# Log-softmax over 50,000 columns: straight code for 512 tiles turned into a hardware loop of 62 rounds over eight fixed buffers

## The chip, the cores and the metric

One core of one Trainium2 chip. The time is that of one execution on the device, in microseconds (us); the core's span in the profile is some 2 us shorter.

## The reference

```
x: [16, 512, 50000] float32
max_x   = max(x, last axis);  shifted = x - max_x
out     = shifted - log(sum(exp(shifted), last axis))
```

8192 rows of 50,000 numbers are read once and written once: 1638 MB in and 1638 MB out. The kernel takes 16 rows as one tile, each row cut into eight pieces, so a tile is 128 partitions x 6250 numbers (3.2 MB); there are 512 tiles.

## The kernel before

The parts that matter, shortened (cuts marked with `...`, loops over halves written in words):

```
NBUF = 8; AHEAD = 7
data = tile_pool(bufs=NBUF)                       # eight buffers of [128, 6250]

def load(t):
    buf = data.tile([P, W]);  nc.sync.dma_start(out=buf, in_=xt[t])          # SP's queue
def front(t):
    nc.vector.reduce_max(out=pmax, in_=buf)       # then four small VectorE steps: row maximum
    ...
    nc.scalar.activation(Exp, two halves of 3125, accum_out=part)            # ScalarE
    nc.tensor.matmul(rowsum, ones, part)          # sum over the eight pieces of a row
    nc.scalar.activation(out=logsum, in_=rowsum, func=Ln)
def back(t):
    nc.vector.tensor_scalar(out=buf, in0=buf, negmax, logsum, add, subtract) # in place
    nc.scalar.dma_start(out=ot[t], in_=buf)                                  # ScalarE's queue

for t in range(AHEAD): load(t)
for t in range(ntiles + 1):
    front(t); back(t - 1); load(t + AHEAD)        # each where it exists
```

VectorE, ScalarE, TensorE and SP are engines of the core, each with a stream of instructions of its own. SP issues the loads and ScalarE the stores; a DMA engine then moves the bytes, and the transfer has landed when its semaphore, a counter that others wait on, has its full count. A store's issue stands in ScalarE's instruction stream, so if it has to wait, ScalarE waits with it.

## Time and profile before

| | before |
|---|---|
| time, median of 6 runs (spread) | 7614.2 us (7614.0 to 7616.0) |
| per tile (span / 512) | 14.87 us |
| DMA share in the middle, GB/s | 1.00, 433 |
| load / store, issue to landing | 51.9 / 37.5 us |
| VectorE, ScalarE busy | 73%, 41% |

In the profile, "DMA share" is the mean busy share of the sixteen DMA engines, and "us to landing" runs from the instruction that issues a transfer to the semaphore that tells of its end. The lines are in the prediction below. The trace also holds a record of every DMA packet (start, length, queue, size), from which I take what no view prints: q1 carries the loads, q10 the stores, packets of 4 bytes, sixteen for each transfer, are the completion writes.

### The profile page before, as it was taken

How to read it: one execution, taken by the hardware profiler on the slowest of the kernel's cores; microseconds unless marked ns; L12 is line 12 of the kernel's file. 1: busy time of each engine (PE TensorE's matmuls, PEld its weight loads, DVE VectorE, ACT ScalarE, POOL GpSimd, SP SyncE). 2: the span in 40 equal slices, each digit the busy share in tenths (PEclk: the TensorE clock that was granted, in tenths of full speed). 3: DMA queues.
4: the chain of work that ended last, by engine and by line, in shares of the span. 5: the costliest groups of instructions: out<-in, count | busy, mean ns of one | idle time of the engine just before them, and what ended most of it. 6: DMA issues, size and time to landing. Idle time of an engine off the chain costs nothing.

```text
span 7612.6 us, 12833 instructions
## 1 busy us (share of the span) xinstructions
PE 600.6 (8%) x2048; PEld 513.2 (7%) x2048; DVE 5567.2 (73%) x3072; ACT 3153.1 (41%) x2561; POOL 1.2 (0%) x7
## 2 busy tenths in 40 slices
PE   0000000000000000000000000000000000000000
PEld 0000000000000000000000000000000000000000
DVE  7777777777777777777777777777777777777776
ACT  4444444444444444444444444444444444444443
POOL 0000000000000000000000000000000000000000
DMA  9999999999999999999999999999999999999998
GB/s 425 433 432 432 432 432 432 432 432 432 432 432 432 432 432 432 432 432 432 432 432 432 432 432 432 432 432 432 432 432 432 432 432 432 431 432 432 432 432 380
DMA packets 147540, 3277.68 MB, mean 431 GB/s; under 512 B 16384, under 2 KB 16384, under 8 KB 16384
## 3 DMA queue, kind: packets, MB, share of 16 engines
q1 hardware_dynamic: 73728, 1638.43, 50.0%
q10 hardware_dynamic: 73728, 1638.43, 50.0%
q14 instruction: 68, 0.56, 0.0%
q8 instruction: 16, 0.26, 0.0%
HBM read 1638.40 MB, written 1638.40 MB: 430 GB/s over the span
## 4 chain that ended last, share of the span: by engine, by line
DVE 73%; another core or an unknown queue 25%; issue 1%; DMA 0%; ACT 0%; PE 0%; ACTq 0%
DVE pmax L81 45%; DVE buf L117 23%; DVE allmax L84 1%; DVE rowmax L86 1%; DVE spread L91 1%; DVE negmax L96 0%; DMA buf<-in_x_dram 0%; ACT dump L102 0%; PE rowsum L108 0%; ACT logsum L112 0%; ACTq L102 0%
## 5 line engine op out<-in xcount | busy, mean ns | idle before, releaser
L81 DVE TENSOR_REDUCE pmax<-buf 128x1 f32<-128x6250 f32 x512 | 3411.8, 6664 | 1953.7 <-DMA buf<-in_x_dram 1953.7
L102 ACT ACTIVATE dump<-buf,negmax 128x3125 f32<-128x3125 f32 x1024 | 2938.1, 2869 | 4092.9 <-DVE negmax L96 4029.5
L117 DVE TENSOR_SCALAR buf<-buf,negmax,logsum 128x6250 f32<-128x6250 f32 x512 | 1789.7, 3496 | 4.5 <-ACT logsum L112 3.6
L108 PE MATMUL rowsum<-part,ones 128*128 128x1 f32 x2048 | 600.6, 363 | 6991.7 <-ACT dump L102 6991.7
L108 PEld LDWEIGHTS rowsum<-part,ones 128*128 128x128 f32 x2048 | 513.2, 311 | 7079.0 <-ACT dump L102 7057.2
L112 ACT ACTIVATE logsum<-rowsum 128x1 f32<-128x1 f32 x512 | 87.6, 171 | 345.8 <-PE rowsum L108 345.8
L102 ACT ACTIVATION_READ_ACCUMULATOR dump<-buf,negmax 128x1 f32 x1024 | 191.1, 187 | 0.0
L96 DVE STREAM_TRANSPOSE negmax<-spread 128x32 f32<-128x32 f32 x512 | 108.2, 211 | 17.7
L84 DVE STREAM_TRANSPOSE allmax<-pmax 128x32 f32<-128x32 f32 x512 | 108.3, 211 | 17.4
L86 DVE TENSOR_REDUCE rowmax<-allmax 128x4 f32<-128x32 f32 x512 | 95.3, 186 | 17.7
L91 DVE COPY spread<-rowmax 128x32 f32<-128x32 f32 x512 | 92.9, 181 | 17.8
L67 ACT ACT_TABLE_LOAD x1 | 1.3, 1283 | 0.8 <-PEq L146 0.8
L59 POOL TENSOR_SCALAR_AFFINE_SELECT ones<-ones 128x128 f32<-128x128 f32 x1 | 0.4, 403 | 0.1
L63 POOL TENSOR_SCALAR_AFFINE_SELECT ones<-ones 128x128 f32<-128x128 f32 x1 | 0.4, 397 | 0.1
L57 POOL MEMSET ones<- 128x128 f32 x1 | 0.2, 204 | 0.3 <-POOLq L146 0.3
L146 POOL MEMSET const-bfloat16-1.0<- 128x1 bf16 x1 | 0.1, 101 | 0.0
L146 POOL MEMSET const-uint8-127<- 128x1 uint8 x1 | 0.1, 101 | 0.0
L146 POOL MEMSET const-float32-0.0<- 128x1 f32 x1 | 0.1, 98 | 0.3 <-issue 0.3
L146 POOL MEMSET const-float32-1.0<- 128x1 f32 x1 | 0.1, 98 | 0.0
## 6 DMA issues: line engine op xcount, KB each, us to landing
buf<-in_x_dram SPq DMA_DIRECT2D x512, 3125.0 KB, 51.9
out_dram<-buf ACTq DMA_DIRECT2D x512, 3125.0 KB, 37.5
```

Of the source, the lines that this page charges most:

```text
L59: nc.gpsimd.affine_select(out=ones3, in_=ones3, pattern=[[-G, R], [0, G]], base=0, channel_multiplier=1, compare_op=ALU.is_ge, fill=0.0,)
L63: nc.gpsimd.affine_select(out=ones3, in_=ones3, pattern=[[G, R], [0, G]], base=G - 1, channel_multiplier=-1, compare_op=ALU.is_ge, fill=0.0,)
L67: nc.scalar.preload_act_table_set("natural_log_exp_and_others")
L81: nc.vector.reduce_max(out=pmax, in_=buf, axis=AX)
L84: nc.vector.transpose(out=allmax, in_=pmax.to_broadcast([P, SQ]))
L86: nc.vector.tensor_reduce(out=rowmax, in_=allmax.rearrange("p (r g) -> p r g", g=G), op=ALU.max, axis=AX, negate=True,)
L91: nc.vector.tensor_copy(out=spread.rearrange("p (r g) -> p r g", g=G), in_=rowmax[:, :, None].to_broadcast([P, SQ // G, G]),)
L96: nc.vector.transpose(out=negmax, in_=spread)
L102: nc.scalar.activation(out=dump, in_=buf[:, j * EXP_C : (j + 1) * EXP_C], func=ACT.Exp, bias=negmax[:, 0:1], scale=1.0, accum_out=part[:, ...
L108: nc.tensor.matmul(rowsum, ones, part[:, j : j + 1], start=j == 0, stop=j == nexp - 1)
L112: nc.scalar.activation(out=logsum, in_=rowsum, func=ACT.Ln)
L117: nc.vector.tensor_scalar(out=buf, in0=buf, scalar1=shift.pop(t)[:, 0:1], scalar2=logs.pop(t), op0=ALU.add, op1=ALU.subtract,)
```

## The change

The intent is a short program: one copy of eight tiles' instructions in a loop, in place of 512 copies, without a barrier between rounds. Its core (the tiles' code moves unchanged, with fixed buffers and single small tiles in place of pools):

```diff
-    data = ... bufs=NBUF        stats = ... bufs=4
+    bufs  = [data.tile([P, W], name=f"buf{j}") for j in range(NBUF)]
+    shift, logs = one small tile per buffer;  pmax, allmax, ... one each
+    def dram(a, t):
+        return a[bass.ds(t, 1)].rearrange("o p w -> (o p) w")     # t may be a register
...
-        nc.sync.dma_start(out=buf, in_=xt[t])
+        nc.sync.dma_start(out=bufs[j], in_=dram(xt, t))
...
-        nc.scalar.dma_start(out=ot[t], in_=buf)
+        nc.scalar.dma_start(out=dram(ot, t), in_=buf)
...
+    def round_of(t, first=False, last=False):
+        for j in range(NBUF):
+            front(j)
+            ...
+            back((j - 1) % NBUF, t + j - 1)
+            load((j - 1) % NBUF, t + j - 1 + NBUF)                # not past the end
-    for t in range(ntiles + 1): ...
+    round_of(0, first=True)
+    with tc.For_i(NBUF, ntiles - NBUF, NBUF, iteration_sync="reg_based") as t:
+        with tc.manual_schedule():
+            round_of(t)
+    round_of(ntiles - NBUF, last=True)
+    back(NBUF - 1, ntiles - 1)
```

## The prediction

> **What bounds the kernel now.** I read the page first: the line of DMA busy tenths, the table of queues, the costliest groups and the DMA issues.
>
> ```profile
> DMA  9999999999999999999999999999999999999998
> q1 hardware_dynamic: 73728, 1638.43, 50.0%
> q10 hardware_dynamic: 73728, 1638.43, 50.0%
> ...
> L81 DVE TENSOR_REDUCE pmax<-buf 128x1 f32<-128x6250 f32 x512 | 3411.8, 6664 | 1953.7 <-DMA buf<-in_x_dram 1953.7
> L102 ACT ACTIVATE dump<-buf,negmax 128x3125 f32<-128x3125 f32 x1024 | 2938.1, 2869 | 4092.9 <-DVE negmax L96 4029.5
> L117 DVE TENSOR_SCALAR buf<-buf,negmax,logsum 128x6250 f32<-128x6250 f32 x512 | 1789.7, 3496 | 4.5 <-ACT logsum L112 3.6
> ...
> buf<-in_x_dram SPq DMA_DIRECT2D x512, 3125.0 KB, 51.9
> out_dram<-buf ACTq DMA_DIRECT2D x512, 3125.0 KB, 37.5
> ```
>
> Loads (q1) and stores (q10) each take 50.0% of the sixteen DMA engines: together all of them, for the whole span. 7612.6 us / 512 tiles is 14.87 us a tile, in which one load and one store of 3.2 MB move. VectorE needs 6.66 + 3.50 us and four small instructions of about 0.2 us, 10.9 us a tile; ScalarE 2 x 2.87 us and small change, about 6.5. Both wait. A load is on its way for 51.9 / 14.87 = 3.5 tiles and a store for 37.5 / 14.87 = 2.5: the DMA engines are full because several transfers stand in each queue at all times.
>
> The waits of the load queue, and a window in the middle, come next:
>
> ```profile
> SPq L75 <- DMA out_dram<-buf: 7305.6, 504, 26.8
> ...
> 4000.00:4100.00 100.00, 7.61 (x26) 6.50 (x26) 73.69 (x42) 42.55 (x33) 0.00 (x0) 1.00 1.00 433
> ```
>
> The load queue always waits for a store to land, since a load takes the buffer of a store. The window's last columns (DMA share 1.00, 433 GB/s) show no idle DMA.
>
> The DMA packet records in the trace give the grain: each transfer is 8 packets of 25,000 bytes on each of 16 engines, a packet takes 928 ns, and a busy engine alternates between q1 and q10. Sixteen packets are 16 x 0.928 = 14.85 us, which is the pace.
>
> Last, how long a transfer takes outside of moving data, from the first load, the first store and the tail (timeline, and the view of the output tensor in the window of the first store):
>
> ```profile
> 0.81 82.23 SPq L75 DMA_DIRECT2D buf<-in_x_dram  x11
> 11.05 6.66 DVE L81 TENSOR_REDUCE pmax<-buf 128x1 f32<-128x6250 f32 x1 [11.05 <-DMA buf<-in_x_dram]
> ```
>
> ```profile
> L121 ACTq DMA_DIRECT2D out_dram<-buf x1: 374/374/374, 32.9 to 32.9; - x1
> ...
> DMA to landing us min/median/max: 20.1/20.1/20.1
> ```
>
> ```profile
> 7592.47 4.05 ACTq L121 DMA_DIRECT2D out_dram<-buf  x2
> ```
>
> The first load, alone, took 11.05 - 0.81 = 10.24 us for 8 x 0.928 = 7.42 us of packets (a cold start). The first store, alone in its queue against a backlog of loads, took 20.1 us. In the tail, with idle engines, the store issued at 7592.47 has its first packet at 7593.31 in the packet records: 0.84 us. The first load's last completion is at 10.68 there and SP issues on it at 11.05; the first store's at 52.74, and SP issues at 53.13: a sequencer reacts to a landing in about 0.4 us.
>
> **What the Trainium skill says.** "DMA: Bandwidth & Descriptors", section "Queues, rings and completion order": an engine round-robins between queue rows at packet granularity. The packet records agree, q1 and q10 alternate. The same page, "Anatomy of one DMA", fits about 2.0 us of fixed cost per transfer (on the GpSimd path) and says that engines never wait on semaphores, the issuing sequencer does. Here I measure 0.84 + 0.4 = 1.24 us warm and 2.8 cold. "Runtime: NRT & Kernel Launch", section "Instruction fetch mechanics": a branch out of the fetched blocks of 256 instructions stalls. No loop body here has 256 instructions on an engine, and ScalarE and VectorE have slack, so no stall should show. "Advanced Engine Details and Errata", "Control Flow Timing", gives about 108 ns for a compare-and-branch; this trace has no branch to check it, and 62 of them are under 7 us even if nothing hid them.
>
> **The change part by part.** The arithmetic, the tile order and the look-ahead (load of tile t+8 once the store of t has landed) are the same. Three things differ.
>
> (1) Loop control: register arithmetic before most waits, and 62 branches per engine. It lies in VectorE's 4 us and ScalarE's 8 us of slack per tile. Instruction fetch falls away (68 packets of 8 KB before). I count 0 us.
>
> (2) Waits on stores. This decides. I read the built program's instruction order with its waits. Before, a store waits for its data and for the store four tiles earlier (the semaphore it reuses). In the loop, the output address comes from a register, and each store waits for the one just before it. The listing on ScalarE, with thresholds from the program:
>
> ```
> store tile t-1 : waits DMAHW0,2,4,6 (all stores of earlier rounds); raises DMAHW0
> store tile t   : waits DMAHW0 >= base+16 (store t-1 landed); raises DMAHW2
> store tile t+1 : waits DMAHW2 >= base+16 (store t landed);   raises DMAHW4
> store tile t+2 : waits DMAHW4 >= base+16; raises DMAHW6
> ```
>
> So only one store is ever in flight, where there were 2.5, and ScalarE, which issues them, stands at each wait.
>
> What a tile then takes: a store lands; ScalarE issues the next store and SP issues a load (it waits for the same landing). Each reaches the engines after 0.4 + 0.84 = 1.24 us. By then the load queue is empty, as I argue: a store now takes longer than 14.85 us from issue to issue, loads get packets in turn with it and all of the gap, so per tile they could move more than the one load that is added; the 3.5 loads of backlog are used up in some ten tiles and the loaded tiles pile up in the buffers. Then one load and one store start together on idle engines and share them, 16 packets, 14.85 us; the store's completion write also has to wait its turn behind the load's last packet. Sum: 1.24 + 14.85 = 16.09 us. I add 0.3 us for what starting from idle costs, my choice: the first load's first packets took 1.3 to 2.3 us instead of 0.93, and packets of engines that start in step took 0.93 to 0.97. That gives 16.4 us a tile. Nothing else is on this path: after issuing a store, ScalarE runs the next tile's exponentials, matmul wait and logarithm in about 7 us while the store flies; VectorE's 10.9 us also fit.
>
> The loop has 62 x 8 = 496 stores. Tile 7's store, the loop's first, should land near 161 us as before (in the old kernel tile 502's landed at 7511, 495 tiles of 14.85 earlier is 161). 161 + 495 x 16.4 = 8279. Some 20 us more for the tiles whose store runs against a backlog (20.1 as the first store did). So the loop's last store lands near 8299.
>
> (3) The loop's end. SP waits there for every transfer of the loop, then all engines meet in a barrier. The last load starts when the last store has landed: 0.4 + 0.84 + 7.5 = 8.7 us with all engines idle, and I allow 3 us for the barrier: 8311. Then eight tiles are left, seven loaded, at VectorE's pace (after the first tiles of the old kernel, 40.37 - 29.45 = 10.92): the maximum of tile 511 is ready after 7 x 10.92 + 7.5 = 84 us. From there the old kernel took 7612.6 - 7585.4 = 27 us to its end, with a straggling DMA engine; I take 23. Total 8311 + 84 + 23 = 8418, rounded to 8400.
>
> **The rivals.** *The loop is free:* the waits on the previous store are met in time, the queues stay full, only the drain at the end costs. Old pace, load 510 issued at 7511, 3.5 loads drain in 26 us, barrier 3, then 84 + 23: about 7650. For it: the DMA engines do the same work, and the change was meant to do this. Against it: stores took 37.5 us at one every 14.87; with one in flight that pace is only possible if a store takes under 14.87 from issue to next issue, and 16 packets alone are 14.85. *The loads fill the gap:* some backlog of loads stays, or stores reach the engines ahead of loads, so that one load packet runs in the gap of 1.24 us: 16.4 - 0.93 = 15.5 us, about 7970. Round-robin with a completion write that waits its turn speaks against it; that both are released by the same landing leaves the order open. *Fixed costs are larger:* 2.0 us as the skill's fit or 2.8 as in the cold first load, 16.9 to 17.7 us a tile: 8650 to 9050. For it: register-addressed transfers may be slower to start, which the old trace can't show; against it the warm 0.84 and 0.4. *ScalarE becomes serial* (exponentials wait for the store too, about 23 us a tile, over 11,000): the order says otherwise, as they come after the issue, not after the landing.
>
> **Range and chances.** The tile time is worth 495 us per us. From 15.7 (gap partly filled) to 17.2 us: 8060 to 8800. The free loop, or a nearly full gap, is all that gives less than 2%; I put 8% on it. Faster by 2% is barred by 512 x 14.85 = 7603 us of packets: 1%.
>
> **What would show it.** In the changed profile: ScalarE's queue waiting for stores to land about 500 times, 8 us or so each; store issue to landing about 16 us in place of 37.5, load about the same in place of 51.9; DMA share about 0.90 and near 390 GB/s all through; VectorE's idle time ended by ScalarE's logarithm, not by loads; VectorE and ScalarE instructions of unchanged length; an end of some 110 us with stores alone. A DMA share of 0.99 in the middle would prove the serial stores harmless, and idle time at each eighth tile alone would mean that the loop's edge, not the store chain, costs.

## The result, and the profile after

9413.7 us median of 6 runs (9407.6 to 9417.2): 1.236 times before, 95% interval 1.235 to 1.238. Ratios in this document are the mean time of one kernel's runs over the mean of the other's runs of the same rounds, so not quite the ratio of the medians. Executions over 1.5% slower than the fastest of the same kernel are left out of the means. The direction and the path were right; the time lies far above the stated range of 8060 to 8800.

The page of the changed kernel, the lines that answer to those of before (busy us and mean ns, then idle time before them and what ended it):

```profile
DMA  9888888888888888888888888888888888888887
...
q1 hardware_dynamic: 73728, 1638.43, 46.6%
q10 hardware_dynamic: 73728, 1638.43, 41.4%
...
L112 DVE TENSOR_SCALAR buf<-buf,negmax,logsum 128x6250 f32<-128x6250 f32 x512 | 1809.2, 3534 | 3623.4 <-ACT logsum L108 3623.4
L87 DVE TENSOR_REDUCE pmax<-buf 128x1 f32<-128x6250 f32 x512 | 3407.7, 6656 | 113.4 <-PEq L162 55.1
...
buf<-in_x_dram SPq DMA_DIRECT2D x512, 3125.0 KB, 18.1
out_dram<-buf ACTq DMA_DIRECT2D x512, 3125.0 KB, 18.3
```

Three things to see. The DMA engines have idle time everywhere, not in one place. Each instruction is as long as before (6656 ns against 6664, 3534 against 3496), so no engine got slower. And VectorE no longer waits for loads (113 us of idle time before its maximum, whatever ended it, against 1953.7): it waits for ScalarE's logarithm. Loaded tiles are there and nobody can go on. A load or a store now lands after 18 us, where they took 51.9 and 37.5: queues that used to hold several transfers hold one.

A window in the middle (the last two columns are DMA share and GB/s):

```profile
4000.00:4100.00 100.00, 5.87 (x20) 5.01 (x20) 60.90 (x35) 31.15 (x26) 0.00 (x0) 1.00 0.86 341
```

One period of the timeline (start, length, engine, line, instruction, idle time before it):

```profile
4006.59 37.41 SPq L83 DMA_DIRECT2D buf<-in_x_dram  x3
4006.61 0.36 ACTq L116 DMA_DIRECT2D out_dram<-buf  x1
4007.23 2.87 ACT L100 ACTIVATE dump<-buf,negmax 128x3125 f32<-128x3125 f32 x1 [11.72 <-DVE negmax L98]
...
4013.92 0.17 ACT L108 ACTIVATE logsum<-rowsum 128x1 f32<-128x1 f32 x1 [0.68 <-PE rowsum L105]
4014.12 3.54 DVE L112 TENSOR_SCALAR buf<-buf,negmax,logsum 128x6250 f32<-128x6250 f32 x1 [7.55 <-ACT logsum L108]
4017.57 6.66 DVE L87 TENSOR_REDUCE pmax<-buf 128x1 f32<-128x6250 f32 x1
...
4025.21 0.36 ACTq L116 DMA_DIRECT2D out_dram<-buf  x1
```

A load and a store leave together at 4006.6; ScalarE does its 7 us of work and is done at 4014.1; then it does nothing until the next store leaves at 4025.21. Note how the profile names the 11.72 us before the exponentials: "DVE negmax". That is the last semaphore the exponentials themselves waited for. What really held ScalarE is the wait in front of the store that stands ahead of them in its stream, and a wait for a landing ahead of a DMA issue is in no engine's busy time. The Trainium skill says something near: "Perfetto Trace Analysis", section "Summary: the profiler window per engine type", has the data movement of a DMA outside the window reported for its instruction. This trace agrees for the instruction (0.36 us for a transfer that takes 18.3), and shows the movement all the same, in the packet records.

Those records tell what the 18.6 us from 4006.6 to 4025.2 are. The old store's last completion write is at 4005.97, the new issues at 4006.6. The sixteen engines begin from 4007.54 on with a load packet each, which takes 2.04 us on the mean in place of 0.93; the first store packets start at 4009.55. From there on load and store packets take turns at 0.93 us. The store's sixteen completions come between 4023.58 and 4024.58.

### The profile page after: what moved, and what is told of

It reads as the page before. It is cut to its first block, busy times and chain, and to the rows that moved or that the text cites. A ratio compares the mean times of both kernels' runs of the same rounds, so it can differ in the third digit from the quotient of the medians.

```text
span 9410.8 us, 21999 instructions
## 1 busy us (share of the span) xinstructions
PE 598.8 (6%) x2048; PEld 513.1 (5%) x2048; DVE 5576.6 (59%) x3072; ACT 3152.2 (33%) x2561; POOL 1.2 (0%) x7
## 5 line engine op out<-in xcount | busy, mean ns | idle before, releaser
L112 DVE TENSOR_SCALAR buf<-buf,negmax,logsum 128x6250 f32<-128x6250 f32 x512 | 1809.2, 3534 | 3623.4 <-ACT logsum L108 3623.4
L87 DVE TENSOR_REDUCE pmax<-buf 128x1 f32<-128x6250 f32 x512 | 3407.7, 6656 | 113.4 <-PEq L162 55.1
L89 DVE STREAM_TRANSPOSE allmax<-pmax 128x32 f32<-128x32 f32 x512 | 108.2, 211 | 17.7
## 6 DMA issues: line engine op xcount, KB each, us to landing
out_dram<-buf ACTq DMA_DIRECT2D x512, 3125.0 KB, 18.3
```

Of the source, the lines that this page charges most:

```text
L87: nc.vector.reduce_max(out=pmax, in_=buf, axis=AX)
L89: nc.vector.transpose(out=allmax, in_=pmax.to_broadcast([P, SQ]))
L112: nc.vector.tensor_scalar(out=buf, in0=buf, scalar1=shift[j][:, 0:1], scalar2=logs[j], op0=ALU.add, op1=ALU.subtract,)
```

## The experiments

I took each period apart in the packet records and issue times (means over tiles 60 to 439, a period being from one store's last completion to the next's; for the loads alone, from load to load):

| us per tile | predicted | changed kernel | e2 straight chain | e4 late load | e7 stores alone | e8 loads alone |
|---|---|---|---|---|---|---|
| landing to next issue | 0.40 | 0.66 | 0.60 | 0.44 | 0.50 | 0.44 |
| issue to that transfer's first packet | 0.84 + 0.93 | 2.87 | 2.88 | 2.64 | 1.17 | 0.94 |
| first packet to its first completion | 13.92 | 14.05 | 14.03 | 11.16 | 7.40 | 8.07 |
| first to last of its 16 completions | 0.30 | 0.85 | 0.83 | 1.58 | 0.35 | 0.91 |
| sum = period | 16.4 | 18.42 | 18.34 | 15.82 | 9.42 | 10.36 |
| first load packet of an engine | 0.93 | 2.01 | 2.00 | 0.99 | - | 1.66 |

(The prediction's sum is split as it was meant: the load's first packet ahead of the store, then fifteen packets; its 0.30 was one lump for starting from idle.)

### The loop with free stores

```diff
+        if not isinstance(t, int): loop_stores.append(...)     # the eight stores of the loop body
...
         with tc.manual_schedule():
             round_of(t)
+        for i, late in enumerate(loop_stores):
+            for early in loop_stores[:i]:
+                tc.declare_no_dep(late, early, query=ANY_SYNC, reason="other rows of out")
+            for other in loop_stores:
+                tc.declare_no_dep(late, other, query=ANY_SYNC, across_iterations=True, reason=...)
```

> The loop as it is, with the store-after-store waits taken out: the eight stores of a round are declared independent of each other, within a round and across rounds (they write different rows), so a store waits only for the store four earlier whose semaphore it reuses, as in the straight kernel. Theory S (each store waits for the one before to land, and that alone costs): about 7655 us, 7635 to 7690; the pace is 14.85 us a tile again, the rest is the drain at the loop's end. Rival L (loop control, register arithmetic, register-addressed transfers cost): stays near 9400 us.

Measured: 7645.2 us, 1.0041 of before (1.002 to 1.006), correct. A fourth run of 7822.3 was slow and isn't used. In the built program each store of the loop again waits only for its data and the store four earlier. The page's DMA issues and the same window:

```profile
buf<-in_x_dram SPq DMA_DIRECT2D x512, 3125.0 KB, 24.0
out_dram<-buf ACTq DMA_DIRECT2D x512, 3125.0 KB, 59.3
```

```profile
4000.00:4100.00 100.00, 7.63 (x27) 6.55 (x27) 73.18 (x42) 42.91 (x34) 0.00 (x0) 1.00 1.00 432
...
7480.00:7520.00 40.00, 0.00 (x0) 0.00 (x0) 0.00 (x0) 0.00 (x0) 0.00 (x0) 1.00 0.70 284
7520.00:7560.00 40.00, 1.76 (x6) 1.50 (x6) 24.32 (x13) 12.13 (x9) 0.00 (x0) 1.00 0.43 172
```

A store takes 59.3 us, four periods, so four are in flight; the DMA engines are full again at 1.00. The loop, its registers and its branches are all still there and cost nothing that shows in the pace. The last two lines are the loop's end: all compute stands still while SP waits for the last transfers, then the DMA engines run short. In the same two windows the kernel before had a DMA share of 1.01 and 0.94.

### The straight kernel with chained stores

```diff
+LANDED = DependencyInfo(DependencyClass.Sync, DependencyReason.DATA)
...
-        nc.scalar.dma_start(out=ot[t], in_=buf)
+        st = nc.scalar.dma_start(out=ot[t], in_=buf)
+        if 7 <= t <= 502:
+            tc.add_manual_dep(st, stores[t - DEPTH].name, LANDED, ...)   # DEPTH = 1
+        stores[t] = st
```

> The straight kernel of before with one thing added: from tile 7 to tile 502 each store waits until the store before it has landed. No loop, no registers. Theory S: about 9400 us, 9250 to 9500 (18.5 us a tile, as in the changed kernel's trace, and no drain). Rival L: 7614 us, unchanged.

Measured: 9323.8 us, 1.2245 of before. No loop, and nearly the whole loss: 1710 of 1800 us. Its issues on the page:

```profile
buf<-in_x_dram SPq DMA_DIRECT2D x512, 3125.0 KB, 18.1
out_dram<-buf ACTq DMA_DIRECT2D x512, 3125.0 KB, 18.3
```

They are those of the changed kernel to the digit. The other 90 us (81 between the two profiled runs) are the loop's: 34 in the pace from tile 7's store, the loop's first, to tile 502's, its last; 14 before (tile 7's store lands at 175.0 in place of 160.5); and 33 after (119 us from tile 502's landing to the end of the span, in place of 86).

### Two stores in flight

The same with `DEPTH = 2`.

> The straight chain, but each store waits for the store two tiles earlier: two stores may be in flight. If what costs is that the engines run empty between a landing and the next store's first packet, a second store in the queue closes that gap: 14.85 us a tile, 7614 to 7680 us. If any wait of a store for an earlier one costs, it stays above 8500 us.

Measured: 7612.3 us, 0.9998 of before (0.998 to 1.001). Its store issues, and the window in the middle:

```profile
out_dram<-buf ACTq DMA_DIRECT2D x512, 3125.0 KB, 29.5
```

```profile
4000.00:4100.00 100.00, 8.21 (x28) 7.02 (x28) 72.51 (x43) 43.09 (x35) 0.00 (x0) 1.00 1.00 432
```

Stores land in 29.5 us, two periods of 14.85. So a wait for an earlier store is not dear by itself; one transfer more in the queue covers it. The loss comes when the queue is empty at each landing.

### The chain with a late load

To the chain: a load also waits for the first half of ScalarE's exponentials of the tile five before it, which start after the store's issue.

```diff
+        if 15 <= t <= 510:
+            tc.add_manual_dep(ld, halves[t - 5].name, LANDED, reason="after the store")
```

So that this half stands earlier in the program, the load's call moves too: `load(t + 5)` comes between `front(t)` and `back(t - 1)`, and eight loads are issued up front. It still waits for the same landing.

> The straight chain, and each load is held back some 3.5 us after the store that it used to start with (it waits for the first half of ScalarE's next exponentials as well). Theory G (the 3.7 us lost per tile are a start from idle engines: 1.6 us of reaction and issue with nothing in flight, then a first load packet of about 2 us ahead of every store, then skew between engines): a store then starts first with packets of 0.93 us, the load's last packets run in the gap after the store's landing: 15.0 to 16.3 us a tile, 7700 to 8350 us. Rival C (each store that waits for a landing costs its tile a constant 3.7 us whatever the loads do): 9400 us or more.

Measured: 8091.2 us, 1.063 of before. The load queue's waits in this kernel (who waited for whom, us in total, times, longest):

```profile
SPq L78 <- DMA out_dram<-buf: 6046.6, 504, 26.6
SPq L78 <- ACT dump L108: 1743.7, 495, 3.8
```

The load is held back 495 times by 3.5 us, and the kernel gains 1233 us by it. The packet records show how. A load that joins engines at work has a first packet of 0.99 us, not 2.01, and what is left of it runs on in the gap after the store's landing: 2.5 load packets on each engine, on the mean, between that landing and the next store's first packet.

The mean of 2.64 us in the table hides two kinds of period, which take turns in most places. In 164 of the 380, the store's first packet comes 0.9 us after its issue, ahead of the load's, and the period is 12.5 us. In 184, the engines still carry a load, that first packet comes 4.3 us after the issue, and the period is 19.1 us; load packets fill the wait, 4.1 on each engine. The load's own first packet comes 4.3 us after its issue as well, on the mean, where it was 0.95 in the changed kernel. Why a transfer that finds the engines with the other direction starts so late was not tested. So the store does not always have its first packets to itself, as I had expected, and 0.97 us a tile over the 14.85 of packets are left.

A wait that is added and saves time shows that the loss is no fixed price of a wait for a landing: it matters when the load arrives.

### Stores in halves

```diff
+        for c in range(2):    # each half waits until the half before it has landed
+            st = nc.scalar.dma_start(out=ot[t][:, c*EXP_C:(c+1)*EXP_C], in_=buf[:, c*EXP_C:(c+1)*EXP_C])
```

> The straight chain with each tile's store in two halves of columns, each half waiting for the half before it to have landed: two waits for a landing per tile, the same bytes. Theory G: the gap between the two halves is filled by the load that is under way, so a tile takes about the same 18 to 19 us: 9100 to 9700 us. Rival C (a constant cost for each wait for a landing): twice 3.7 us, 22 us a tile, about 11200 us.

Measured: 10129.1 us, 1.330 of before: neither. The timeline says why:

```profile
4005.59 12.55 ACTq L124 DMA_DIRECT2D out_dram<-buf  x2
...
4018.25 2.87 ACT L104 ACTIVATE dump<-buf,negmax 128x3125 f32<-128x3125 f32 x1 [12.54 <-DMA out_dram<-buf]
...
4024.94 0.17 ACT L114 ACTIVATE logsum<-rowsum 128x1 f32<-128x1 f32 x1 [0.68 <-PE rowsum L110]
4025.00 12.90 ACTq L124 DMA_DIRECT2D out_dram<-buf  x2
```

The two halves leave at 4005.6 and about 4017.8. The second half's completions are in by 4023 in the packet records, but ScalarE is at its exponentials until 4024.94 and only then issues the next first half. SP, whose load waits for the same landing, issues it 2 us sooner, so the engines have load packets in hand when the first half comes, and it takes about 12 us; the second half then runs with no load beside it. Here ScalarE's own work got onto the path, which I had not seen, and the load filled no gap. The run tells the two theories apart in neither direction.

### Each direction by itself

Both wrong: one direction keeps whole transfers, chained one after the other, the other direction and the compute touch 64 of 6250 columns.

> Wrong result on purpose: whole tiles are loaded for the first eight only, then 64 of 6250 columns, and the compute touches those 64 columns; the stores are whole and chained one after the other. It measures a chained store with no load of size beside it. From the changed kernel's trace: 0.6 reaction + 0.95 issue + 8 packets of 0.93 (7.4) + 0.3 skew = 9.2 to 9.4 us a tile, 4650 to 4800 us in all; were the whole 3.6 us of loss a cost of the store by itself: 11 us a tile, 5550 us.

> Wrong result on purpose, the mirror: loads whole and chained one after the other (each waits for the load before it to land), stores and compute of 64 columns. If a load that starts on idle engines has a first packet of 2.0 us instead of 0.93 wherever it stands: 0.5 + 0.95 + 2.0 + 7 x 0.93 + 0.3 = 10.2 us a tile, about 5150 us. If the long first packet is only what a load and a store do to each other: 9.2 us, about 4650 us.

Measured: 4859.9 us and 5262.3 us (one run each, state unknown). The whole transfers on their pages, e7's and then e8's:

```profile
out_dram<-buf ACTq DMA_DIRECT2D x512, 3125.0 KB, 9.2
```

```profile
buf<-in_x_dram SPq DMA_DIRECT2D x512, 3125.0 KB, 10.3
```

A chained store takes 9.42 us a tile, 2.0 over its packets. That is just above the 9.2 to 9.4 that I expected (the small load's packets come first: issue to first store packet 1.17 in place of 0.95); most of what the 4859.9 lie above 4800 is outside the pace, in 194 us before tile 7's landing and after tile 502's. A chained load takes 10.36 us, 2.9 over its packets: its first packets take 1.66 us with no store packet beside them, and its completions spread by 0.91 us where the store's spread by 0.35. So the long first packet belongs to a load that starts on idle engines; beside a store it is 2.01, and the store pays for it, since it stands behind. The spread may belong to it too (0.85 beside a store), but here the 32 KB stores run into the load's end, so that is not shown cleanly. Why a load's first packet is slow on idle engines stays open.

### The loop's code, unrolled

```diff
-    with tc.For_i(NBUF, ntiles - NBUF, NBUF, iteration_sync="reg_based") as t:
-        with tc.manual_schedule():
-            round_of(t)
+    for t in range(NBUF, ntiles - NBUF, NBUF):
+        round_of(t)
```

> The changed kernel with a Python loop in place of the hardware loop: straight code, but eight fixed buffers, single small tiles and eight loads up front as in the change. These parts cost nothing by my theory: 7600 to 7620 us; then the 31 us that the loop with free stores takes over before are the loop's end. If they cost, about 7645 us.

Measured: 7615.7 us, 1.0001 of before. Fixed buffers, single small tiles and eight loads up front cost nothing, so the 29 us by which the loop with free stores stands above this kernel are the loop's. They are not in its pace: from landing to landing of the stores (tiles 59 to 439) it takes 14.851 us a tile, against 14.865 unrolled and 14.859 before. They lie at its edges: tile 7's store, the loop's first, lands at 175.2 in place of 157.2, and from tile 502's landing, the loop's last, to the end of the span are 121.4 us in place of 101.1. In between the loop is 11 us quicker (7346.7 against 7357.6); why was not tested.

## Why the prediction was wrong, point by point

**What bounds the kernel before, and the rival of a free loop.** Right. Full queues made the pace; with the stores freed the loop takes 7645 us, where the rival said about 7650.

**Part 1, loop control costs nothing.** Right for the pace, to within 0.1 us a tile: the loop with free stores keeps 14.85 us; the chained loop is 0.08 us a tile above the chained straight code. Not foreseen: the loop's first store lands 14 to 18 us later than in the straight code of the same kind. The prediction has it at 161 us, as before (it was 156.7 there; the 161 came of taking 14.85 for 14.858 a tile); it landed at 175.0. The 20 us for tiles that run against a backlog happen to cover that, which is luck.

**Part 2, one store in flight, ScalarE stands at each wait.** Right, shown from both sides: taking the waits out of the loop gives back all but 31 us of 1800, putting them into straight code costs 1710 us. Also right: the load queue runs empty, load and store start together, nothing of the compute is on the path.

**Part 2, the sum of a tile: here it failed.** The step is "I add 0.3 us for what starting from idle costs, my choice", with the 1.24 us before it. The period is 18.42 us, not 16.4; 495 x 2.02 = 1000 us of the miss of 1014. By terms: the reaction took 0.66 in place of 0.40 and the issue 0.95 in place of 0.84 (0.37 together); the first load packet, ahead of the store on all engines, took 2.01 in place of 0.93 (1.0 on the store's path); fifteen more packets 14.05 in place of 13.92; and the sixteen completions spread over 0.85, for which there was only what the 0.3 left (0.55 more). I had the number for the largest of these in hand: I quote first packets of 1.3 to 2.3 us from the first load (not quite alone, as I wrote: five more stood behind it), called it a cold start, and then allowed 0.3 us, a third of the 1.0 that it costs here. In the old kernel that start happens once; in the new one it happens 496 times. The figures 0.4 and 0.84 came from the few places where the old kernel's queues were not in this state: its landings were watched while other transfers ran, its quick issue was a store into idle engines, not a load.

**The rival with larger fixed costs** named 2.0 and 2.8 us (16.9 to 17.7 us a tile) and I argued it down with the warm numbers. The truth lay beyond it: 3.57 us over the packets.

**The rival of a filled gap** did not happen by itself, but the late load makes it happen in part: 15.82 us a tile and 8091 us, where the rival said 15.5 and 7970.

**Part 3, the loop's end.** Right: from the last completion of the loop's last store (9291.6, predicted 8299) to the end of the span are 119 us, predicted 119. By its parts as well: 11.3 us until VectorE goes on, at 9302.9 (predicted 12), and 108 from there (predicted 107).

**What the profile would show.** Store and load landing at nearly the same time, VectorE waiting for the logarithm, unchanged instructions: seen. The DMA share was 0.86 to 0.89 and not 0.90, 341 to 351 GB/s and not 390; landing took 18 us and not 16. ScalarE's wait shows in the timeline (11.7 us, not 8), but the profile books it under the exponentials' semaphore, not under a landing.

No version tried beats both kernels. For a short program the loop with free stores is the one to take, at 0.4% over straight code.

## What to carry to other kernels

A loop with register addresses can bring in waits that straight code doesn't have: here each store to the output came to wait for the one before it, and declaring them independent took the wait away. Read the waits in the built program, and declare the stores independent where they are, or see that a second transfer stands in the queue (two stores in flight were enough here).

When a change empties a queue that used to be full, take the start-up costs from a place in the trace where the same transfers start from idle together, and multiply them by how often that will now happen. A number measured on a queue at work need not hold there: a load's first packet took 0.93 us in the old kernel's full queue and 2.01 in the new one's empty one.

## What the Trainium skill lacked or had wrong

- "DMA: Bandwidth & Descriptors", section "Anatomy of one DMA", gives about 2.0 us of fixed cost, fitted on the GpSimd path, and lays most of it to completion. For transfers issued by ScalarE and SP the runs show 2.0 us for a store by itself (9.42 - 7.42) but 2.9 us for a load (10.36 - 7.42) and 3.57 us for a load and a store that start together (18.42 - 14.85), where 2.01 us are the load's first packet on idle engines, 0.93 in full queues. Each of these sums includes 0.44 to 0.66 us from a landing to the next issue. The page's fit has no difference by direction, and no slow first packet of a load on idle engines.
- The same page, section "Queues, rings and completion order", has the round-robin, which held once both queues had packets going; it doesn't say that a store issued at the same moment as a load starts behind the load's slow first packet (2.87 us after its issue), that a transfer which finds the engines with the other direction can start 4.3 us after its issue, nor that holding the load back 3.5 us can gain time (9323.8 to 8091.2 us).
- No page among those read tells that stores with register addresses to one tensor are chained in a loop: 1.236 times the time here, 1.004 when declared independent.
